# High weight tiles before low ones in each quadrant product, and query pieces cut early and used

## The chip, the cores and the metric

The kernel runs on one core of one Trainium2 chip. The metric is the device time of one execution in microseconds, as the median of several runs. TensorE (PE) multiplies matrices, and each matmul has a load of its own for its stationary operand (PEld in the profile). VectorE (DVE) and ScalarE (ACT) do element-wise work, GpSimd (POOL) a little, and SyncE (SP) issues the DMA transfers.

## The reference

A decoder trunk of two layers on 512 tokens with 1024 channels, batch 1, all in float32. Layer 0 mixes with multi-head latent attention (MLA), layer 1 with gated linear attention (GLA). Each mixer is followed by an MLP with a squared ReLU, and a last RMS norm ends the trunk:

```python
def sq_relu_mlp(xn, w_up, w_down):
    hid = jnp.square(jax.nn.relu(xn @ w_up))
    return hid @ w_down

# layer i:  x += Mixer_i(rms_norm(x));  x += sq_relu_mlp(rms_norm(x), w_up, w_down)
# w_up is 1024 x 4096, w_down 4096 x 1024
```

The GLA mixer begins with `h = rms_norm(x) @ w_in`, and the first 512 columns of `h` are its queries.

## The kernel before, in words

**Layout.** The residual stream lies transposed in SBUF: `xT[j]` holds channels 128j to 128j+127 on the partitions and the 512 tokens along the row. `first` and `second` are the token halves of 256.

**Split precision.** A float32 product is made of three matmuls in a reduced format. An operand is split into a high and a low part: `split` (L108) writes the high part as a rounded copy on ACT (L110) and the low part as source minus high part on DVE (L113). `mm3` (L115) issues high weight x high input (L118), high weight x low input (L119) and low weight x high input (L120), one after the other. `piece` (L143) makes such a pair of weight tiles, `wh` and `wl`, of 1024 columns; there are three buffers of each.

**The MLP.** Its products are made by a scheme in the manner of Strassen. The input is cut into quadrants, by channel half and token half, and each 2 x 2 block product takes seven quadrant products instead of eight. The sums and differences of quadrants that this needs are made by `QuadNorm.pair` (L281) for the normed input (its four results T1 to T4 for one pair of channel tiles), by DVE subtractions and additions on the weights, and by additions on the results. The weights go up in 8 blocks of 512 columns. `up_block` (L811) returns its steps: `s1` is the product named 11, `s2` is 21 on top of it, `s5` is T1, `s6` T2, `s3` 22, `s7` T3 and `s4` T4. Block 0 has a step `s0` that loads and cuts its first weights before the MLP begins. An up product is 4 k tiles x 2 output tiles x 3 = 24 matmuls of 256 columns into the two halves of one PSUM bank. Its loop has the output tile outside and k inside. `down_block` (L928) does the same for the way down, for the first 6 blocks: a down product is 4 k tiles x 4 output tiles x 3 = 48 matmuls, fed by two weight pieces; its input is split on the spot (`operand`, L937). `matmuls` (L797) is the loop of both. The last two blocks go down by plain products of 512 columns (`down`, L1024, or `down_final`, L1039).

**The order around the MLP.** `out_proj` (L769) closes the mixer: four steps, each with two output tiles, whose results are added to the residual (L783), scaled, split, squared and paired for the MLP. In its last step it lets the MLP run its first step `s0`. Then the MLP itself starts: two matmuls that only warm up, then the lead, which is the steps `s1`, `s2` of block 0 and `s1`, `s2` of block 1. Behind the first of them `begin` (L1077) puts the norm (`finish`, L251: one product with `acc`, the sum of squares, in float32, L253, then a reciprocal root on ACT and DVE) and four subtractions on `xT` (L1080). Behind the lead come the other steps, with down products put between them. Block 1 reads its first weights by one DMA of 1 MB into the pool `down_w` (L824), the others by DMAs of 512 KB (L829), all issued by SP.

**The GLA's start.** While the last piece of the MLP's last block is being used, `prefetch` (L1547) loads the weights of the GLA's first 256 query columns and cuts two pieces into `self.qk`. Nothing reads them. `gla` then calls `proj_qk(0)` (L1189), which loads the same columns again (L1190) and cuts them (L1191). `a_pair` (L389) multiplies: 8 k steps of 6 matmuls, with the norm issued before the sixth step. After it come the second projection, the scales per token (eight tiny matmuls, L1216) and the gates.

**What sets the order.** The program is traced in the order of the code; a scheduler then orders the instructions of each engine by priority and by what it reckons to be ready, so the matmuls of two products may be mixed. `tc.keep_in_program_order(i)` ties an instruction to the program's order on its engine, and `with tc.issue_after(i)` puts what the block traces behind `i` on `i`'s engine. Waits on data and on free buffers are added by the framework. `PADS` are unused bytes at the start of a pool, which shift the addresses behind them. Down in memory, pools that are opened after others are closed take over their space, and a tile waits for those whose bytes it takes.

## Time and profile before

| What | Value |
|---|---|
| Median of 3 runs | 1106.01 us (1104.63 to 1106.75) |
| Profiled execution | 1105.17 us, its span 1103.5 us |
| TensorE busy | 1071.4 us, 97% of the span, 7322 matmuls |
| VectorE busy | 895.1 us, 81% |
| ScalarE busy | 643.1 us, 58% |
| Mean granted TensorE clock | 0.988 |
| HBM read and written | 106.74 MB, 2.10 MB |

In a row of groups stand the line, the engine, the operation, what it writes and reads, shapes and count, then busy time and the mean of one in ns, then the idle time of the engine just before them with what ended it. A row of waits has the engine and line that waited, what it waited for, the total, the number of times and the longest. A row of the timeline has start, duration, engine, line, operation and operands, and in brackets the idle time before it with what ended it. A matmul's duration is longer than its distance to the next, as matmuls overlap; the pace is read from the starts. The 512-column matmuls of the mixers and the 256-column ones of the MLPs lie in different stretches: the MLPs run from about 190 to 475 us and from 762 to 1049 us, the GLA from about 519 us.

### The profile page before, as it was taken

How to read it: one execution, taken by the hardware profiler on the slowest of the kernel's cores; microseconds unless marked ns; L12 is line 12 of the kernel's file. 1: busy time of each engine (PE TensorE's matmuls, PEld its weight loads, DVE VectorE, ACT ScalarE, POOL GpSimd, SP SyncE). 2: the span in 40 equal slices, each digit the busy share in tenths (PEclk: the TensorE clock that was granted, in tenths of full speed). 3: DMA queues.
4: the chain of work that ended last, by engine and by line, in shares of the span. 5: the costliest groups of instructions: out<-in, count | busy, mean ns of one | idle time of the engine just before them, and what ended most of it. 6: DMA issues, size and time to landing. Idle time of an engine off the chain costs nothing.

```text
span 1103.5 us, 17836 instructions
## 1 busy us (share of the span) xinstructions
PE 1071.4 (97%) x7322; PEld 985.7 (89%) x7322; DVE 895.1 (81%) x1212; ACT 643.1 (58%) x936; POOL 44.5 (4%) x78
## 2 busy tenths in 40 slices
PE   8999999899999999998899999999999999999997
PEld 7788988899999999986688888887999999999986
DVE  6789878999899899867365654678899899799865
ACT  6576654566567676645234744655556566766734
POOL 6410000000000000030000000000000000000000
PEclk9999999999999999999799999999999999999999
DMA  7312113523432523250222212223423523422312
GB/s 215 83 48 77 39 46 99 181 78 115 154 103 90 184 85 100 92 192 0 86 77 77 77 40 76 77 77 124 145 96 99 170 77 126 154 86 95 128 45 77
DMA packets 100098, 109.98 MB, mean 100 GB/s; under 512 B 8129, under 2 KB 74961, under 8 KB 100017
## 3 DMA queue, kind: packets, MB, share of 16 engines
q1 hardware_dynamic: 98000, 107.62, 30.8%
q10 hardware_dynamic: 1952, 1.21, 0.4%
q8 instruction: 57, 0.93, 0.4%
q0 software_dynamic: 64, 0.02, 0.1%
q14 instruction: 25, 0.20, 0.1%
HBM read 106.74 MB, written 2.10 MB: 99 GB/s over the span
## 4 chain that ended last, share of the span: by engine, by line
PE 85%; DVE 10%; ACT 2%; issue 1%; DMA 0%; ACTq 0%; DVEq 0%
PE ps L118 26%; PE ps L120 26%; PE ps L119 26%; DVE wl L113 3%; PE ps L135 2%; PE ps L1342 2%; ACT wh L110 1%; DVE raw L1000 1%; DVE h L113 1%; DVE raw L884 1%; DVE set L244 1%; DVE acc L236 1%; PE ps L1379 0%; DVE raw L899 0%; PE ps L666 0%
## 5 line engine op out<-in xcount | busy, mean ns | idle before, releaser
L110 ACT ACTIVATE wh<-raw 128x1024 fp32r<-128x1024 f32 x210 | 221.4, 1058 | 180.5 <-PE ps L119 141.5
L113 DVE TENSOR_TENSOR wl<-raw,wh 128x1024 fp32r<-128x1024 f32 x210 | 255.5, 1224 | 25.4 <-ACT wh L110 24.9
L120 PE MATMUL ps<-h,wl 128*128 128x256 f32 x672 | 188.5, 281 | 2.2 <-DVE wl L113 2.2
L118 PE MATMUL ps<-h,wh 128*128 128x256 f32 x672 | 188.1, 280 | 0.0
L119 PE MATMUL ps<-h,wh 128*128 128x256 f32 x672 | 188.0, 280 | 0.0
L120 PEld LDWEIGHTS ps<-h,wl 128*128 128x128 f32 x672 | 126.5, 188 | 3.1 <-DVE wl L113 3.0
L118 PEld LDWEIGHTS ps<-h,wh 128*128 128x128 f32 x672 | 126.4, 188 | 0.0
L119 PEld LDWEIGHTS ps<-h,wh 128*128 128x128 f32 x672 | 126.4, 188 | 0.0
L110 ACT ACTIVATE wh<-wraw 128x1024 fp32r<-128x1024 f32 x43 | 44.8, 1055 | 85.2 <-PE ps L120 41.5
L118 PE MATMUL ps<-set,wh 128*128 128x512 f32 x232 | 92.7, 400 | 1.6 <-ACT set L243 1.6
L119 PE MATMUL ps<-set,wh 128*128 128x512 f32 x232 | 92.5, 399 | 0.1
L120 PE MATMUL ps<-set,wl 128*128 128x512 f32 x232 | 92.3, 398 | 0.0
L113 DVE TENSOR_TENSOR wl<-wraw,wh 128x1024 fp32r<-128x1024 f32 x43 | 52.6, 1229 | 10.8 <-ACT wh L110 10.6
L118 PE MATMUL ps<-wh,set 128*128 128x512 f32 x144 | 59.7, 414 | 0.0
L841 ACT ACTIVATE q<-q 128x512 f32<-128x512 f32 x64 | 40.1, 626 | 30.7 <-DVE q L840 30.7
L113 DVE TENSOR_TENSOR h<-q,h 128x1024 fp32r<-128x1024 f32 x42 | 51.4, 1224 | 7.9 <-ACT h L110 7.9
L120 PE MATMUL ps<-wh,set 128*128 128x512 f32 x144 | 56.3, 391 | 0.0
L119 PE MATMUL ps<-wl,set 128*128 128x512 f32 x144 | 56.2, 391 | 0.0
L118 PEld LDWEIGHTS ps<-set,wh 128*128 128x128 f32 x232 | 44.5, 192 | 10.7 <-ACT set L243 1.8
L119 PEld LDWEIGHTS ps<-set,wh 128*128 128x128 f32 x232 | 44.8, 193 | 9.9 <-DVE set L244 0.8
L120 PEld LDWEIGHTS ps<-set,wl 128*128 128x128 f32 x232 | 44.7, 193 | 9.3
L110 ACT ACTIVATE h<-q 128x1024 fp32r<-128x1024 f32 x42 | 44.1, 1049 | 0.8 <-DVE q L986 0.8
(490 smaller groups left out, 3005.8 us busy)
## 6 DMA issues: line engine op xcount, KB each, us to landing
raw<-in_mlp_w_down_dram SPq DMA_DIRECT2D x38, 1024.0 KB, 5.1
raw<-in_mlp_w_up_dram SPq DMA_DIRECT2D x62, 512.0 KB, 3.9
wraw<-in_gla_w_in_dram SPq DMA_DIRECT2D x12, 1024.0 KB, 5.1
wraw<-in_mla_w_o_dram SPq DMA_DIRECT2D x8, 512.0 KB, 4.8
wraw<-in_gla_w_o_dram SPq DMA_DIRECT2D x8, 512.0 KB, 4.8
raw<-in_mlp_w_up_dram SPq DMA_DIRECT2D x2, 1024.0 KB, 7.6
xT<-in_x_dram SPq DMA_DIRECT2D x6, 256.0 KB, 7.4
wraw_qn<-in_mla_w_uq_dram SPq DMA_DIRECT2D x6, 256.0 KB, 3.4
```

Source lines behind the costliest of these rows:

```text
L110: order(ACT.activation(hi, src, AF.Copy))
L113: lo_eng.tensor_tensor(lo, src, f(hi), ALU.subtract)
L118: PE.matmul(psum, wh, xh, start=start, stop=False, **kw)
L119: PE.matmul(psum, wh, xl, start=False, stop=False, **kw)
L120: PE.matmul(psum, wl, xh, start=False, stop=stop, **kw)
L135: PE.transpose(psum, src, ident[: src.shape[0], : src.shape[0]])
L236: DVE.tensor_tensor(self.acc, self.acc, s, ALU.add)
L244: DVE.scalar_tensor_tensor(lo, src, g, f(hi), ALU.mult, ALU.subtract)
L841: ACT.activation(qs, qs, AF.Square)
L884: DVE.tensor_tensor(s, v["a21"], v["a22"], ALU.add)
L1000: DVE.tensor_tensor(v["S"], v["12"], v["S"], ALU.subtract)
L1342: PE.matmul(p[:, t * 64 : (t + 1) * 64].rearrange("p (n c) -> p n c", c=m), k[:, sl], later, start=True, stop=True)
```

## The change

It has these parts, all around the two MLPs and the start of the GLA:

- **Order in a quadrant product.** `matmuls` issues all matmuls with the high weight tile first, for each k and output tile the high and the low input, and then all with the low weight tile. An up product goes through both output tiles inside k, where it finished one output tile first. A down product does so for each of its two pieces.
- **Products in program order.** The first matmul of each such group is kept in program order.
- **The lead.** The last pair of channel tiles is combined (`pair(3)`) not at the end of `out_proj` but in block 1's first step, behind the cut of that step's weights. The norm goes from behind block 0's `s1` into its `s2`, before that result is finished, with its matmul kept in order. The four subtractions go behind the lead. Block 1's first weights are loaded before the lead, by two DMAs of 512 KB instead of one of 1 MB.
- **Helpers.** `split` returns its DVE instruction, and `piece` keeps it in the list `cut_at`.
- **The GLA.** `proj_qk(0)` uses the two pieces that `prefetch` cut; the second load and cut are gone.
- **A pad** of 224 bytes in front of the pool `down_w`.

```diff
-    PADS = dict(stage=224, right=64, up=448, masks=256, keep=128)
+    PADS = dict(stage=224, right=64, up=448, masks=256, keep=128, down_w=224)
...
+    cut_at = []
...
-        split(raw, hi, lo, order=order)
+        cut_at.append(split(raw, hi, lo, order=order))
...
-            nxt.pair(c)
+            if c < 3:
+                nxt.pair(c)
...
-            for k in ks:
-                for m in ms:
-                    mm3(
...
+            def one(i, j, k, m, start, stop):
+                return PE.matmul(
+                    p[:, m * TH : (m + 1) * TH],
+                    w[i][:, k - k0, m * P : (m + 1) * P],
+                    x[k][j],
...
+            steps = [(k, m) for k in ks for m in ms]
+            for k, m in steps:
+                i = one(0, 0, k, m, begin and k == 0 and m % 2 == 0, False)
+                if (k, m) == steps[0]:
+                    tc.keep_in_program_order(i)
+                one(0, 1, k, m, False, False)
+            for k, m in steps:
+                one(1, 0, k, m, False, end and k == 3)
...
                 if b == 1 and half == 0:
...
+                    return ahead[trail]
...
-                for j in range(2):
-                    matmuls(p, w, 0, range(KH), [j], quad[name], begin, True)
+                matmuls(p, w, 0, range(KH), range(2), quad[name], begin, True)
...
+                if b == 1:
+                    v["11"] = piece(a, KH, 256)
+                    with tc.issue_after(cut_at[-1].ins):
+                        nrm.pair(KH - 1)
                 product(v["x1"], a, "11", True)
...
                 product(v["x1"], v["a12"], "21", False)
+                if b == 0:
+                    nrm.finish(tc.keep_in_program_order)
                 finish(pairs(v["x1"]), 0, first)
...
-        opened("down_w")
+        pad(opened("down_w"), PADS["down_w"])
...
+        t = wide_raw().rearrange("p a (b n) -> p (a b) n", b=2)
+        ahead = t[:, :KH], t[:, KH:]
+        for i, a in enumerate(ahead):
+            SP.dma_start(a, w_up[i * 512 : i * 512 + 512, FB : FB + 256].rearrange("(k p) n -> p k n", p=P))
         lead = [blocks[b].pop(0) for b in (0, 0, 1, 1)]
-        for i, step in enumerate(lead):
+        for step in lead:
             step()
-            if i == 0:
-                begin()
+        with tc.issue_after(cut_at[-1].ins):
+            for k in range(KH):
+                DVE.tensor_tensor(xT[k][:, second], xT[k][:, second], xT[k + KH][:, second], ALU.subtract)
...
-            raw = col_chunk(w_in, c * 256, 256)
-            w = [piece(raw[:, :, j * P : (j + 1) * P], ND, P) for j in range(2)]
+            if c == 0:
+                w = nrm.qk
+            else:
+                raw = col_chunk(w_in, c * 256, 256)
+                w = [piece(raw[:, :, j * P : (j + 1) * P], ND, P) for j in range(2)]
```

More of the change, by code (lines that the diff above doesn't have):

```diff
@@ L249, in add, with finish @@
             self.square(src)
-        def finish(self):
+        def finish(self, order=lambda i: i):
             m = bank("c")
-            PE.matmul(m, self.inv, self.acc, start=True, stop=True)
+            order(PE.matmul(m, self.inv, self.acc, start=True, stop=True))
             r = sb.tile([P, S], F32, tag="rstd", bufs=1, name=uname("rstd"))
@@ L1075, in down_final @@
                         nxt.row(t, c, ps_[c])
-        def begin():
-            nrm.finish()
-            for k in range(KH):
-                DVE.tensor_tensor(xT[k][:, second], xT[k][:, second], xT[k + KH][:, second], ALU.subtract)
         blocks = [up_block(b) for b in range(NB)]
```

19 lines of the change are left out of this document (5 added, 14 removed).

## The prediction, on record before the changed kernel was run

> **What bounds the kernel now.** I read the page first, then TensorE's waits, then the stretches round each place that the change touches.
>
> ```profile
> PE 1071.4 (97%) x7322; PEld 985.7 (89%) x7322; DVE 895.1 (81%) x1212; ACT 643.1 (58%) x936; POOL 44.5 (4%) x78
> ...
> PE 85%; DVE 10%; ACT 2%; issue 1%; DMA 0%; ACTq 0%; DVEq 0%
> ...
> L113 DVE TENSOR_TENSOR wl<-raw,wh 128x1024 fp32r<-128x1024 f32 x210 | 255.5, 1224 | 25.4 <-ACT wh L110 24.9
> ```
>
> TensorE (PE) is the bound, and where the chain of work that ended last leaves it, it goes through VectorE (DVE, 10%), mostly to make the low weight tile `wl`, 1.22 us each. The matmuls' waits, in total us, times, longest:
>
> ```profile
> PE ps L120 <- DVE wl L113: 7.4, 7, 1.8
> PE ps L253 <- DVE acc L236: 4.3, 1, 4.3
> PE ps L118 <- ACT wh L110: 3.6, 4, 1.0
> PE ps L1216 <- DVE rstd L219: 3.6, 1, 3.6
> ```
>
> L120 is the low-tile matmul: it waits for the very thing that the new order asks for later. L253 and L1216 are the norm and the token scales at the start of the GLA. The stretches, in order the length, busy time (and instructions) of PE, its weight loads, DVE, ACT, POOL, then the granted clock:
>
> ```profile
> 190.40:244.30 53.90, 48.97 (x390) 47.04 (x389) 49.00 (x53) 30.60 (x39) 0.00 (x0) 0.97 0.46 149
> 762.20:816.50 54.30, 49.06 (x389) 47.04 (x389) 49.32 (x54) 30.48 (x39) 0.00 (x0) 0.97 0.45 146
> 244.30:475.10 230.80, 228.52 (x1971) 227.91 (x1970) 216.79 (x197) 154.01 (x174) 5.37 (x10) 1.00 0.36 115
> 816.50:1048.90 232.40, 230.73 (x1970) 230.00 (x1970) 216.32 (x196) 154.81 (x175) 0.00 (x0) 1.00 0.36 116
> 275.00:300.00 25.00, 25.00 (x220) 25.00 (x220) 22.20 (x20) 15.28 (x19) 0.00 (x0) 1.00 0.52 169
> 975.00:1000.00 25.00, 24.95 (x213) 24.75 (x212) 24.25 (x22) 16.59 (x19) 0.00 (x0) 1.00 0.39 125
> 518.70:543.90 25.20, 17.33 (x57) 13.11 (x57) 9.54 (x13) 6.91 (x11) 0.00 (x0) 0.73 0.20 53
> ```
>
> The first two rows are the leads of the two MLPs (from the first up product to the first down product), the next two the rest of them. An undisturbed stretch does 220 matmuls of 256 columns in 25 us, 113.6 ns each; another only 213, 117.4 ns. A lead holds 16 products of 24 such matmuls: 16 x 24 x 113.6 ns = 43.6 us, with the norm and two warming matmuls some 44.6. The leads are 9.3 and 9.7 us longer than that. The rest has 42 up and down products per MLP, 1968 matmuls, 223.6 us at that pace: 7.2 and 8.8 us over. The last row is the GLA's start: 25 us at 17.3 busy and a mean clock of 0.73. These are the places where anything can be won. DVE is busy 94% of the third row, so it is nearly a second bound.
>
> **The change part by part. GLA start.** Today the query pieces are cut during the last down product and thrown away; the projection loads and cuts them again.
>
> ```profile
> 507.87 1.06 ACT L110 ACTIVATE wh<-raw 128x1024 fp32r<-128x1024 f32 x1
> ...
> 510.56 1.05 ACT L110 ACTIVATE wh<-raw 128x1024 fp32r<-128x1024 f32 x1
> ...
> 526.49 1.04 ACT L110 ACTIVATE wh<-wraw 128x1024 fp32r<-128x1024 f32 x1
> ...
> 521.65 0.75 DVE L244 SCALAR_TENSOR_TENSOR set<-xT,gains,set 128x512 fp32r<-128x512 f32 x1 [0.79 <-ACT set L243]
> ...
> 496.06 0.39 PE L120 MATMUL ps<-hh,wl 128*128 128x512 f32 x1
> ...
> 518.50 0.39 PE L120 MATMUL ps<-hh,wl 128*128 128x512 f32 x1
> 523.15 2.05 PE L253 MATMUL ps<-acc,inv 128*128 128x512 f32 x2 [4.25 <-DVE acc L236]
> 528.81 1.86 PE L1216 MATMUL ps<-one_t,rstd 1*128 1x1 f32 x8 [3.62 <-DVE rstd L219]
> ...
> 531.19 0.63 PE L119 MATMUL ps<-set,wh 128*128 128x512 f32 x1
> 531.62 0.63 PE L118 MATMUL ps<-set,wh 128*128 128x512 f32 x1
> ...
> 543.73 0.39 PE L118 MATMUL ps<-set,wh 128*128 128x512 f32 x1
> ```
>
> The pieces at 507.87 and 510.56 are the unused ones; the used ones are cut at 526.49, behind the norm, and PE, with the projection ordered behind norm and scales, stands still after 518.7 and then runs at 430 ns a matmul. Full pace is (518.50 - 496.06) / 99 intervals = 227 ns. With the early pieces the 48 query matmuls can start at 518.7: the sixth of eight k steps comes 6.8 us later with the norm before it, and the last token tile (521.65 + 0.75 = 522.4) is there. 518.7 + 48 x 0.227 + 0.75 for the norm (193.61 to 194.36 in the lead) = 530.4, against 543.73: 13.3 us. The scales (1.86) come later instead: 11.5 sure, 13.3 at best. **I take 12.** The pieces now hold two of three `wh` buffers till 530.4; the second must wait until the last but one down piece frees its own, about 513. The next projection's first piece finds the buffer freed at 518.7 and its second is cut while 24 matmuls (5.4 us) run: nothing added. The dropped 1 MB load and two cuts were hidden and free 2.4 us of DVE.
>
> **The leads.** Here are moved: the cut of block 1's first piece ahead of the last T tile (`pair(3)`: two ACT, five DVE instructions), the norm behind block 0's second product, four subtractions behind the lead, and block 1's load (now two DMAs) ahead of block 0's second pair.
>
> ```profile
> 187.91 0.39 SPq L824 DMA_DIRECT2D raw<-in_mlp_w_up_dram  x1
> ...
> 190.67 0.69 DVE L783 TENSOR_TENSOR xT<-ps,xT 128x512 f32<-128x512 f32 x1 [1.19 <-PE ps L120]
> ...
> 195.00 0.48 DVE L290 SCALAR_TENSOR_TENSOR raw<-xT,gains,raw 128x256 f32<-128x256 f32 x1
> ...
> 197.00 1.23 DVE L113 TENSOR_TENSOR T3l<-raw,T3h 128x1024 fp32r<-128x1024 f32 x1
> ...
> 199.47 1.22 DVE L113 TENSOR_TENSOR wl<-raw,wh 128x1024 fp32r<-128x1024 f32 x1
> ...
> 193.61 1.12 PE L253 MATMUL ps<-acc,inv 128*128 128x512 f32 x2
> 194.36 0.49 PE L118 MATMUL ps<-x4h,wh 128*128 128x256 f32 x1
> ...
> 198.49 0.39 PE L118 MATMUL ps<-x0h,wh 128*128 128x256 f32 x1 [0.93 <-ACT wh L110]
> ...
> 200.75 0.39 PE L120 MATMUL ps<-x0h,wl 128*128 128x256 f32 x1 [1.75 <-DVE wl L113]
> ```
>
> The piece waited for at 198.49 and 200.75 stands behind `T3l` at 199.47 on DVE. Its DMA is out at 187.91 and SP holds nothing in front of it that it must pass but the second pair's load; both land before PE asks (two first products, 190.7 + 5.7 + 0.75 = 197). Cut first, its low tile can be ready near 194.5, and both waits go. Late next is `T3l`: four short DVE instructions like the one at 195.00 and its own 1.23, some 3 us, due in the last k quarter of T1's high half, which begins after four products: 190.5 + 4 x 2.8 + 0.75 = 202.5, so near 204. If that cover failed, T1 would wait for it, at most 2 us. The bounds: nothing, or PE's 9.3. But DVE works 49.0 of 53.9 us there, so the lead shortens by its idle 4.9, by the 1.1 of a cut put into the idle 1.19 before 190.67, and by what the low tiles are asked for later (after 16 matmuls instead of 2, 14 x 0.1136 = 1.6): 7.6 at most. Part of that idle is DVE waiting for ACT. **I take 6 each, 12 in all.**
>
> **The order inside a product.** A product keeps its 24 or 48 matmuls and weight loads. In the rest of the MLPs the waits are like this one:
>
> ```profile
> 355.02 0.28 PE L119 MATMUL ps<-T0l,wh 128*128 128x256 f32 x1
> 356.04 0.39 PE L120 MATMUL ps<-T0h,wl 128*128 128x256 f32 x1 [0.75 <-DVE wl L113]
> ```
>
> The start is 1.02 us late where 0.11 is due, after a wait of 0.75: some 0.27 for the restart. Of the seven L120 waits two of up to 1.75 are in the leads; five remain with 7.4 - 3.5 = 3.9 us, with restarts 5.3. The 1.6 us of slack covers each alone; as DVE is 94% busy some come back. From 0 to 5.3, **I take 4.4.** `wh` is also let go after two thirds of a product, so ACT's copies, which are no bound (58%), start earlier.
>
> Against it stands the pace. Up products run all of one output half and then the other; after the change they alternate halves, as down products do after every three matmuls. A down and an up product side by side, in undisturbed time (48 and 24 matmuls; the counts hold some that overlap the edges):
>
> ```profile
> 291.31:296.92 5.61, 5.61 (x51) 5.61 (x50) 3.00 (x3) 2.69 (x4) 0.00 (x0) 1.00 0.67 233
> 296.92:299.64 2.72, 2.72 (x27) 2.72 (x25) 2.52 (x3) 2.01 (x2) 0.00 (x0) 1.00 0.85 265
> ```
>
> 116.9 ns and 113.3 ns. Over both MLPs, 4704 matmuls outside and inside the leads, all at 113.6 instead of the present 116 or so (230.80 less 3 of stalls over 1968) would win 10; all at 117.4 would lose 6. **I take a loss of 2.5**, near the down row. The `down_w` padding moves addresses only; the matmul kept in order per product issues nothing.
>
> **Sum.** The profiled execution took 1105.17 us for a span of 1103.5; the median is 1106.01, 0.8 above it. 1105.2 - 12 - 12 - 4.4 + 2.5 = 1079.3; on the median 1080.1, so **1080**.
>
> **The rivals.** *DVE is the bound.* The leads and later waits come back as DVE waits elsewhere, and only the GLA start stays: 1106 - 12 + 0 to 2 = 1095. For: 49.0 of 53.9 and 216.79 of 230.80 us busy. Against: 14 us idle in that long stretch, so work can be caught up.
>
> *The early pieces don't free PE.* The norm and scales are still put ahead of the queries, PE waits till 530.6 and only the cut is gone; then about 1.5 of the 12 stays: 1090. For: today's order. Against: that order has the pieces cut late, and these are cut by 514.
>
> *The pace falls with the order.* With a new weight address and another half at each low matmul the stream slows; this is the case that ends slower. The gains are 28.4, so over 4704 matmuls it decides from 6 ns more, 122 ns or 205 in 25 us; at 200 in 25 us, 125 ns, the time is 1106 - 28.4 + 4704 x 9 ns = 1120. For: 213 against 220 shows that the pace isn't fixed. Against: loads are one for each matmul already (7322 of both), and switching halves costs at most 3.6 ns in the down row.
>
> *The pace rises* to 113.6 throughout, with fewer disturbances: 1106 - 28.4 - 10 = 1068. The Trainium skill (TensorE: Matmul & The Clock Gate, Back-to-back issue gap) gives 262 cycles of 2.4 GHz for 256 columns, 109 ns: by that the same case would end about 1047. No row here is under 113.
>
> **How the numbers follow.** Forecast 0.62, DVE-bound 0.15, pieces late 0.09, pace up 0.08, pace down 0.04, and 0.02 for a mix of the bad ones near no change. The forecast's own terms (GLA 11.5 to 13.3, leads 4 to 15, waits 0 to 5.3, pace -10 to +6) make 1068 to 1092 likely; with the DVE case inside, **1066 to 1095** leaves some 2 in 10 out. Faster, by over 0.2% (2.2 us, about what a measurement tells from no change), in all but the last two: 0.94; same 0.01; slower 0.05.
>
> **What would show it.** The query matmuls begin by 519 without a wait, at 227 ns, and the norm stands between them. PE has no wait for `wl` over 0.3 us in block 1's first product, and a lead shrinks to 46 to 50 us. The total of L120's waits falls under 3 us. In a stretch after the lead 25 us hold 213 to 217 matmuls. Wrong are the steps if the leads stay near 54 us with DVE full, if the norm still precedes the queries, or if quiet stretches hold under 210.

## The result

The changed kernel takes **1095.91 us** (median of 4 runs, 1095.63 to 1096.2) against 1105.6 for the kernel before on the same chip: ratio 0.9916, 95% interval 0.99 to 0.9932. That is 9.7 us faster; 26 were forecast. The profiled execution took 1096.2 us, with a span of 1094.5.

The page of the changed kernel, its line of engines, its chain and the group of the low weight tiles:

```profile
PE 1070.8 (98%) x7322; PEld 988.7 (90%) x7322; DVE 891.5 (81%) x1210; ACT 641.7 (59%) x934; POOL 44.1 (4%) x78
...
PE 90%; DVE 5%; ACT 2%; DMA 2%; issue 1%; SPq 0%; DVEq 0%; ACTq 0%
...
L113 DVE TENSOR_TENSOR wl<-raw,wh 128x1024 fp32r<-128x1024 f32 x210 | 253.9, 1218 | 25.5 <-ACT wh L110 24.5
```

The same view of TensorE's waits (total us, times, longest):

```profile
PE ps L802 <- DVE q L926: 6.0, 4, 1.9
PE ps L802 <- ACT wh L110: 3.3, 2, 1.6
PE ps L802 <- ACT mt L876: 1.5, 2, 0.7
PE ps L802 <- ACT ps L882: 1.3, 2, 0.7
...
PE ps L802 <- DVE wl L113: 0.9, 2, 0.5
```

The waits for `wl` fell from 7.4 to 0.9 us, and those of the norm and the scales (4.3 and 3.6) are gone. But there are new ones: the T4 products, which follow T3 in the program's order and go into the same bank, wait for the sum `q` that still reads it (L926), and others wait for evacuations and high tiles on ACT. L802 is every matmul of the MLP products now.

The same stretches as before: both leads, both rests, the first 25 us of the queries, two quiet stretches (length; busy time and instructions of PE, weight loads, DVE, ACT, POOL; granted clock):

```profile
191.56:247.46 55.90, 49.43 (x389) 47.72 (x388) 48.92 (x56) 31.25 (x40) 0.00 (x0) 0.97 0.28 86
753.53:808.10 54.57, 48.00 (x390) 46.21 (x389) 48.75 (x56) 31.02 (x40) 0.00 (x0) 1.00 0.29 88
247.46:479.24 231.78, 231.78 (x1971) 231.78 (x1970) 216.33 (x197) 154.53 (x175) 5.43 (x8) 1.00 0.36 114
808.10:1039.87 231.77, 231.77 (x1971) 231.77 (x1969) 216.33 (x196) 155.38 (x176) 0.00 (x0) 1.00 0.36 117
522.79:547.79 25.00, 25.00 (x112) 19.58 (x111) 14.49 (x20) 8.93 (x13) 0.00 (x0) 1.00 0.19 53
300.00:325.00 25.00, 25.00 (x215) 25.00 (x214) 23.63 (x23) 15.83 (x17) 0.00 (x0) 1.00 0.38 119
900.00:925.00 25.00, 25.00 (x215) 25.00 (x214) 24.90 (x23) 17.49 (x20) 0.00 (x0) 1.00 0.30 86
```

Set against the stretches that the prediction shows:

| stretch | before | after | difference |
|---|---|---|---|
| up to the first MLP | 190.47 | 191.56 | +1.1 |
| first lead | 53.90 | 55.90 | +2.0 |
| rest of the first MLP | 230.8 | 231.8 | +1.0 |
| plain down part, GLA, to the second MLP | 287.0 | 274.3 | -12.8 |
| second lead | 54.3 | 54.6 | +0.2 |
| rest of the second MLP | 232.4 | 231.8 | -0.6 |
| what is left | | | +0.1 |
| span | 1103.5 | 1094.5 | -9.0 |

The GLA's start gave all that was forecast, and the granted clock there is 1.00 where it was 0.73. The 1.1 us ahead of the first MLP arise near 15 us of the span, in a wait of 0.9 us behind the first loads, which the change does not touch; over all traces of this study that part takes 190.5 to 193.2 us. The leads did not shrink at all. In the rests PE is busy without a gap (231.78 of 231.78), so every wait is gone, and yet they take as long as before. These two are the questions for the experiments.

The granted clock bears on the leads. In the changed kernel's first lead (0.97) one wait is followed by a stretch at half the clock, in which matmuls start some 213 ns apart where 118 ns is usual:

```profile
221.94 0.39 PE L802 MATMUL ps<-T0h,wh 128*128 128x256 f32 x1 [1.89 <-DVE q L926]
...
222.70 0.42 PE L802 MATMUL ps<-T1h,wh 128*128 128x256 f32 x1
222.92 0.41 PE L802 MATMUL ps<-T1l,wh 128*128 128x256 f32 x1
223.13 0.41 PE L802 MATMUL ps<-T1h,wh 128*128 128x256 f32 x1
```

The stretch is 3.41 us long, so it costs some 1.7 us, and the second lead has none (1.00). Before, each lead had one (0.97 in both rows of the prediction), at the wait of 1.75 us for `wl`. In the leads of all the traces such a stretch begins within 1.5 us of the end of a PE wait of 1.6 to 2.9 us, but waits of up to 2.5 us bring none in other leads; what decides it, no run here shows. So the length of a lead has to be read together with its clock.

The query matmuls stand directly behind the last down matmul, and the norm (L255) stands between them:

```profile
522.56 0.39 PE L120 MATMUL ps<-hh,wl 128*128 128x512 f32 x1
522.79 0.39 PE L118 MATMUL ps<-set,wh 128*128 128x512 f32 x1
...
529.36 0.39 PE L120 MATMUL ps<-set,wl 128*128 128x512 f32 x1
529.59 1.02 PE L255 MATMUL ps<-acc,inv 128*128 128x512 f32 x2
530.05 0.80 PE L118 MATMUL ps<-set,wh 128*128 128x512 f32 x1
```

### The profile page after: what moved, and what is told of

It reads as the page before. It is cut to its first block, busy times and chain, and to the rows that moved or that the text cites. A ratio compares the mean times of both kernels' runs of the same rounds, so it can differ in the third digit from the quotient of the medians.

```text
span 1094.5 us, 17834 instructions
## 1 busy us (share of the span) xinstructions
PE 1070.8 (98%) x7322; PEld 988.7 (90%) x7322; DVE 891.5 (81%) x1210; ACT 641.7 (59%) x934; POOL 44.1 (4%) x78
## 4 chain that ended last, share of the span: by engine, by line
PE 90%; DVE 5%; ACT 2%; DMA 2%; issue 1%; SPq 0%; DVEq 0%; ACTq 0%
PE ps L802 47%; PE ps L118 12%; PE ps L119 12%; PE ps L120 12%; PE ps L1356 2%; PE ps L135 1%; DVE wl L113 1%; DMA wraw_ckv<-in_mla_w_in_dram 1%; ACT wh L110 1%; DMA raw<-in_mlp_w_up_dram 1%; PE ps L1393 0%; DVE q L845 0%; PE ps L1362 0%; PE ps L1342 0%; PE ps L668 0%
## 5 line engine op out<-in xcount | busy, mean ns | idle before, releaser
L802 PE MATMUL ps<-h,wh 128*128 128x256 f32 x1344 | 172.2, 280 | 0.0
L802 PEld LDWEIGHTS ps<-h,wh 128*128 128x128 f32 x1344 | 164.5, 188 | 0.0
L802 PE MATMUL ps<-h,wl 128*128 128x256 f32 x672 | 92.7, 280 | 0.0
L802 PEld LDWEIGHTS ps<-h,wl 128*128 128x128 f32 x672 | 85.1, 188 | 0.0
L113 DVE TENSOR_TENSOR wl<-wraw,wh 128x1024 fp32r<-128x1024 f32 x41 | 50.3, 1229 | 10.7 <-ACT wh L110 10.5
L119 PEld LDWEIGHTS ps<-set,wh 128*128 128x128 f32 x232 | 44.0, 190 | 10.7 <-DVE set L246 1.6
L802 PE MATMUL ps<-T0h,wh 128*128 128x256 f32 x128 | 33.8, 287 | 9.3 <-DVE q L926 6.0
L118 PE MATMUL ps<-hh,wh 128*128 128x512 f32 x96 | 37.4, 389 | 0.0
```

The costliest lines, as they stand in the source:

```text
L113: return lo_eng.tensor_tensor(lo, src, f(hi), ALU.subtract)
L118: PE.matmul(psum, wh, xh, start=start, stop=False, **kw)
L119: PE.matmul(psum, wh, xl, start=False, stop=False, **kw)
L802: return PE.matmul(p[:, m * TH : (m + 1) * TH], w[i][:, k - k0, m * P : (m + 1) * P], x[k][j], start=start, stop=stop, skip_group_check=True,)
```

## The experiments

Three theories were put against each other. *Order*: the new order inside the products, or the rule that products keep the program's order, costs PE time in the leads and slows its pace. *DVE*: DVE bounds the leads, as a rival in the prediction has it. *Arrangement*: the moved pair, norm and transfers make the leads longer. A ratio is always to the kernel before, with its 95% interval. The spacing of quiet matmuls is worked out from their start times, all intervals under 135 ns from the first down product on. The runs lie on several chips and at several times, where the kernel before took 1103.8 to 1106.5 us; two times of different runs are therefore compared by their ratios too.

### The parts, one by one

**The early pieces alone**, on the kernel before:

```diff
+            if c == 0:
+                w = nrm.qk
```

> The kernel before with one edit alone: the first query projection uses the pieces that the prefetch cut. Theory: this is the whole of the gain; TensorE goes from the last down product straight to the query matmuls, 12 to 13 us less, so 1093, which would be faster than the changed kernel by 2 to 3 us, and the rest of the change costs that. Rival: the GLA's start wins only in company with the new order; 1100 or more.

1092.18 us, ratio 0.9883 (0.9866 to 0.99). In its trace the way from the last down matmul to the second MLP takes 230.8 us (519.55 to 750.31) against 243.5 (518.73 to 762.24) before. The pieces alone are worth as much as forecast, and alone they are faster than the whole change, by 3.7 us, though the two intervals touch. So the rest of the change costs time.

**The changed kernel without the pieces:**

```diff
-            if c == 0:
-                w = nrm.qk
```

> The changed kernel without the early query pieces: the first projection loads and cuts its own weights again behind the norm. With the pieces alone the kernel before gained 14 us (12 were forecast). If that holds in company of the rest too, 1106 to 1112, above the kernel before; if the new order makes the GLA's start shorter by itself, 1098 to 1104.

1109.38 us, ratio 1.0028 (1.0015 to 1.0041): 13.5 us above the changed kernel (12.4 by the ratios), and slower than before. The waits of the kernel before are back:

```profile
PE ps L255 <- DVE acc L238: 4.3, 1, 4.3
PE ps L1227 <- DVE rstd L221: 3.6, 1, 3.6
```

The GLA term stands, with or without the other parts.

**The changed kernel without the program order of products:**

```diff
-                if (k, m) == steps[0]:
-                    tc.keep_in_program_order(i)
```

> The changed kernel without keeping each product's first matmul in program order; all else stays. Theory 'order': in the lead of the changed kernel T4 stands right behind T3 and waits for the sum at L926 that reads T3's bank (1.89 and 1.06 us in the first MLP, 6.0 us in all four); set free, other products' matmuls fill these waits, the two leads shrink from 55.9 and 54.6 us to 52 or less, and the time falls by 4 to 6 us. Rival 'DVE': the lead ends when VectorE's 49 us of work and its own waits are through; the leads stay within 1 us, and so does the time.

1095.77 us, ratio 0.9913 (0.9895 to 0.9931); leads 55.65 and 54.30, spacing 117.64 and 117.90 ns. Nothing changes: the kept program order is not the cause.

**The changed kernel with the old order inside the products** (high, high, low of each k step), the rest kept:

```diff
-            steps = [(k, m) for k in ks for m in ms]
+            up = len(ms) == 2
+            steps = [(k, m) for m in ms for k in ks] if up else [(k, m) for k in ks for m in ms]
...
-            for k, m in steps:
                 one(1, 0, k, m, False, end and k == 3)
```

> The changed kernel with the old order inside a product (high-high, high-low, low-high for each tile, up products one half after the other), first matmul still in program order. Theory 'order sets the pace': undisturbed up products go back from 2.82 to 2.72 us and down products from 5.66 to 5.61, and the waits for the low tile come back with some 6 us; the time stays within 3 us of the changed kernel's. Rival 'state': the pace is a state that the stream falls into at its start and keeps when nothing disturbs it; products stay at 2.83 until a wait comes, and the time rises by 4 us or more.

1104.08 us, ratio 0.9978 (0.9966 to 0.999): the high-first order is worth some 8 us in company of the rest. The leads grow by 3 and 3.6 us (58.83 and 58.21, the granted clock 0.94 in both, so some 1.7 and 3.4 us of it are the clock) and waits return to the rest. The spacing is 116.5 and 116.6 ns in up products and 116.8 and 117.0 in down products, so the pace depends on the order too, by about 1 ns. The order theory has lost half of its ground: the new order helps.

**The same with the products free to move:**

```diff
-                if (k, m) == steps[0]:
-                    tc.keep_in_program_order(i)
```

> The changed kernel with the old order inside the products and without the wait for the program's order: the new lead and the pieces alone. If the new lead costs by itself, leads of 56 us or more and 1094 to 1100 us, above the 1092.2 of the pieces alone. If it was the program order that made the three-by-three run dear (1104.1, leads near 58.5), the leads come back to 54 and the time to about 1092.

1100.88 us, ratio 0.9948 (0.9932 to 0.9965): 8.7 us above the pieces alone (7.2 by the ratios). New lead and old order together cost.

**High first, but one output half after the other:**

```diff
+            steps = [(k, m) for m in ms for k in ks] if up else [(k, m) for k in ks for m in ms]
```

> The changed kernel, high tiles still first, but in up products one output half after the other within the high and within the low part; down products unchanged. Theory 'halves': alternating the output half is what slows the stream, so up products go from 2.82 to 2.72 us while down products stay at 5.66, and the time falls by 8 to 10 us. Rival 'low tiles in a row' or 'state': up products stay at 2.82, and the time stays within 1 us.

1095.21 us, ratio 0.991 (0.9891 to 0.9928). The spacing is 117.3 in up and 116.7 in down products: the change of halves is not what makes the up products slow.

**The kernel before with pieces and high-first order, old lead** (this loop without the program order):

```diff
+            for k, m in steps:
+                one(0, 0, k, m, begin and k == 0 and m % 2 == 0, False)
+                one(0, 1, k, m, False, False)
+            for k, m in steps:
+                one(1, 0, k, m, False, end and k == 3)
```

> The kernel before, with the early query pieces and the high-first order inside the products; the lead, the transfers and the free order stay those of before. If the new lead arrangement is what costs (the sum, the late pair and the program order on DVE and PE), this run keeps the 14 us of the pieces, loses the waits for wl (some 4 us) and shows leads near 51 us: 1082 to 1088 us. If the high-first order itself slows the quiet matmuls (117.6 ns against 113.6 in the up products), it gains the waits and gives them back: 1091 to 1095 us with up spacing near 117.6.

1084.5 us, ratio 0.9796 (0.9771 to 0.9822): 11 us faster than the whole change. The leads are 51.54 and 54.19 (clock 1.00 and 0.97); the up products run at 117.8 ns in the first MLP and at 114.1 in the second. So high-first does not need the new lead, and it does not force the slow pace throughout.

**The changed kernel with all three parts of the lead undone** (pair, norm with its subtractions, transfers; program order kept), the edits of the next three runs together:

```diff
-            if c < 3:
-                nxt.pair(c)
+            nxt.pair(c)
...
+                nrm.finish()
...
-                    return ahead[trail]
```

> The changed kernel with all three parts of the lead undone (pair, norm and subtractions, transfers), so only the pieces, the high-first order and the program order of the products are left. Against the 1084.5 of the same without the program order: if the program order costs, 1089 to 1096; if it costs nothing, 1082 to 1088.

1085.2 us, ratio 0.9831 (0.9813 to 0.985). Not to be told from the run without the program order, as the intervals overlap; leads 52.13 and 52.13, the clock 1.00 in both. **The arrangement of the lead costs 10.7 us** (9.4 by the ratios).

### Which part of the arrangement

**The pair back at its old place:**

```diff
-            if c < 3:
-                nxt.pair(c)
+            nxt.pair(c)
...
-                    with tc.issue_after(cut_at[-1].ins):
-                        nrm.pair(KH - 1)
```

> The changed kernel with the fourth pair of the norm where it stood before (ahead of the lead, not behind block 1's first pieces). The kernel with the old lead and the high-first order took 1084.5, the changed one 1095.9: 11 us that the lead's new arrangement must have cost, in the lead (4.4 us in the first MLP) and in the quiet pace (117.6 against 113.6 in the up products). If the late pair is what does it, 1086 to 1090 and a lead under 53 us in the first MLP; if it is not, 1094 to 1098.

1089.44 us, ratio 0.9869 (0.9843 to 0.9895). More than half of it, but not all. Leads 53.34 and 54.90 (clock 1.00 and 0.97), and the pace is no longer fixed: 117.8 ns in the up products of the first MLP, 114.3 in those of the second.

**Norm and subtractions back:**

```diff
-                if b == 0:
-                    nrm.finish(tc.keep_in_program_order)
...
-        for step in lead:
+        for i, step in enumerate(lead):
             step()
-        with tc.issue_after(cut_at[-1].ins):
-            for k in range(KH):
+            if i == 0:
+                nrm.finish()
+                for k in range(KH):
```

> The changed kernel with the norm's scale and the four subtractions of the second half of xT straight behind the lead's first step, as before. If moving these is the cause, 1086 to 1090; if it is not, 1094 to 1099 (the subtractions then stand ahead of the lead's sums on DVE, as in the kernel before).

In this kernel the late fourth pair reads its second half after the subtractions, so the numbers in its tiles differ; the instructions are the same. 1093.08 us, ratio 0.9895 (0.9874 to 0.9915), leads 53.11 and 54.55 (clock 1.00 and 0.97), spacing 117.64 and 117.90 as in the changed kernel. A small part, between the two expectations.

**The transfers back:**

```diff
-                    return ahead[trail]
+                    if not trail:
+                        t = wide_raw().rearrange("p a (b n) -> p (a b) n", b=2)
+                        SP.dma_start(t, w_up[:, c0 : c0 + 256].rearrange("(k p) n -> p k n", p=P))
+                        v["a12"] = t[:, KH:]
+                    return t[:, :KH]
```

> The changed kernel with block 1's first tile loaded in one transfer from within the block, as before, in place of two transfers ahead of the lead. If the place of these transfers matters, 1086 to 1092; if not, 1095 to 1097.

1101.01 us, ratio 0.9968 (0.9955 to 0.9982): slower by 5.1 us, which neither expectation has. With the late pair, the early transfers are needed.

**Pair and norm back, transfers kept early:**

```diff
-            if c < 3:
-                nxt.pair(c)
+            nxt.pair(c)
...
+                nrm.finish()
```

> The changed kernel with pair and norm (with its subtractions) where they were, but block 1's transfers still ahead of the lead. Undoing only the transfers made it slower by 5.1 us; undoing all three parts made it 10.7 us faster. If the early transfers are good in themselves, this is faster than the 1085.2 with all three undone: 1078 to 1084. If their worth came from the late pair and norm alone, 1084 to 1088.

1084.45 us, ratio 0.9806 (0.9783 to 0.9829). The transfers by themselves bring nothing that can be told from the 1085.2 without them. This is, with the old lead above, the fastest kernel of the study: 11 us below the changed one, 21 below the one before.

The leads of these kernels in the same view. The first lead with the pieces alone, and with all three parts undone:

```profile
191.39:245.58 54.19, 48.95 (x390) 46.97 (x388) 49.12 (x53) 30.50 (x39) 0.00 (x0) 0.97 0.45 147
...
190.67:242.80 52.13, 47.94 (x389) 46.27 (x388) 49.49 (x54) 31.14 (x40) 0.00 (x0) 1.00 0.48 153
```

With pair and norm back, transfers early:

```profile
190.89:242.58 51.69, 47.14 (x389) 45.69 (x388) 49.49 (x54) 31.15 (x40) 0.00 (x0) 1.00 0.48 155
747.40:799.06 51.66, 47.14 (x389) 45.68 (x388) 49.48 (x54) 31.13 (x40) 0.00 (x0) 1.00 0.48 155
```

The changed kernel with the transfers back:

```profile
193.12:251.15 58.03, 50.87 (x390) 48.90 (x389) 48.78 (x56) 31.03 (x40) 0.00 (x0) 0.94 0.27 83
757.24:815.15 57.91, 50.55 (x390) 48.52 (x389) 48.78 (x56) 31.03 (x40) 0.00 (x0) 0.94 0.26 82
```

DVE works 48.8 to 49.5 us in every one of them. What differs is how long it idles: 2.2 us with pair and norm back, 7.0 and 5.8 in the changed kernel, 9.2 with the transfers back. With pair and norm early, the lead is as long as DVE's work and little more. PE's idle time is 4.5 us with pair and norm back, 6.5 and 6.6 in the changed kernel, 7.2 and 7.4 with the transfers back. The rest of the difference is mostly the clock: with the transfers back it is 0.94 in both leads, which costs some 3.4 us each. The changed kernel has 0.97 and 1.00, so the clock is most of what the one with the transfers back loses against it in the leads. Where DVE idles in the changed kernel stands in its timeline (start, length, instruction, in brackets the idle time before it and what ended it):

```profile
193.49 0.75 DVE L276 SCALAR_TENSOR_TENSOR x7l<-xT,gains,x7h 128x512 fp32r<-128x512 f32 x1 [0.79 <-ACT x7h L275]
194.16 0.69 DVE L238 TENSOR_TENSOR acc<-acc,tmp 128x512 f32<-128x512 f32 x1
196.40 1.23 DVE L113 TENSOR_TENSOR wl<-raw,wh 128x1024 fp32r<-128x1024 f32 x1 [1.55 <-ACT wh L110]
...
199.80 0.48 DVE L292 SCALAR_TENSOR_TENSOR raw<-xT,gains,raw 128x256 f32<-128x256 f32 x1
201.63 0.69 DVE L218 SCALAR_TENSOR_TENSOR mt<-ps,mt 128x512 f32<-128x512 f32 x1 [1.35 <-ACT mt L129]
...
205.11 1.22 DVE L113 TENSOR_TENSOR T3l<-raw,T3h 128x1024 fp32r<-128x1024 f32 x1
```

And ACT, which ended these three idle times and twice stood behind PE itself:

```profile
194.82 0.58 ACT L882 ACTIVATE ps<-ps 128x512 f32<-128x512 f32 x1 [0.84 <-PE ps L802]
195.31 2.00 ACT L110 ACTIVATE wh<-raw 128x1024 fp32r<-128x1024 f32 x2
199.44 0.69 ACT L129 ACTIVATE mt<-ps,eps_t 128x512 f32<-128x512 f32 x1 [2.13 <-PE ps L255]
```

With the pair early, DVE has its work there (`raw`, the sums, `T3l` at 197.42) and no idle time from 191.8 to 204:

```profile
193.89 0.48 DVE L291 SCALAR_TENSOR_TENSOR raw<-xT,gains,raw 128x256 f32<-128x256 f32 x1
194.28 1.22 DVE L890 TENSOR_TENSOR raw<-raw,raw 128x1024 f32<-128x1024 f32 x1
195.42 0.48 DVE L292 SCALAR_TENSOR_TENSOR raw<-xT,gains,raw 128x256 f32<-128x256 f32 x1
195.82 0.48 DVE L293 SCALAR_TENSOR_TENSOR raw<-xT,gains,raw 128x256 f32<-128x256 f32 x1
196.21 1.22 DVE L918 TENSOR_TENSOR raw<-raw,raw 128x1024 f32<-128x1024 f32 x1
197.42 1.22 DVE L113 TENSOR_TENSOR T3l<-raw,T3h 128x1024 fp32r<-128x1024 f32 x1
```

So the piece that is "cut first" is not cut sooner: ACT makes its high tile only behind the evacuation of the first product (L882, 194.82), and DVE, whose filler was moved away, stands idle for 3.7 us. That work then comes on top, later. DVE's subtraction for T2 (L910) begins at 208.42, 16.9 us into the lead; in the kernel before it began at 204.20, 13.7 us into it. ACT can cut T2's high tile only behind that and behind the evacuation of T1, at 210.19. So PE waits inside T1 and ahead of T2, where neither the kernel before nor the one with pair and norm back has a wait:

```profile
208.44 0.50 PE L802 MATMUL ps<-T0h,wl 128*128 128x256 f32 x2 [0.47 <-DVE wl L113]
...
211.29 0.39 PE L802 MATMUL ps<-T0h,wh 128*128 128x256 f32 x1 [1.63 <-ACT wh L110]
```

The waits for `q` (2.9 us in this lead) are no part of the difference: they are 2.9 us with pair and norm back as well.

**Does DVE bound the changed lead?** Its eight sums in each lead are left out (the products then run on tiles as loaded):

```diff
-                DVE.tensor_tensor(s, v["a21"], v["a22"], ALU.add)
+                if b > 1:
+                    DVE.tensor_tensor(s, v["a21"], v["a22"], ALU.add)
```

(likewise the three subtractions in `s6`, `s3` and `s7`)

> The changed kernel without the eight sums of weight tiles on DVE in each lead (of blocks 0 and 1, some 1.22 us each, 9.8 us of DVE): this leaves out part of the computation, the products of the lead run on tiles as loaded. If DVE, 88% busy there, is what keeps the changed lead at 55.9 and 54.6 us, the leads come down to 48 to 50 us and the time to 1082 to 1087. If it is the places of the pieces and evacuations in the order, PE waits as long without the sums: leads of 53 us or more and 1091 to 1096.

1089.83 us, ratio 0.9852 (0.983 to 0.9874); leads 51.72 and 51.69, between the two expectations. The lead gets 4.2 and 2.9 us back, 1.7 of the first by the clock (1.00 in both). DVE's work inside it falls by 6.5 and 6.4 us of the 9.8, to 42.4. DVE is thus part of the bound and not all of it: PE, busy 47.6 us of the 51.7, then still waits, most of all for the sums of results and for evacuations.

### The pace

**A short matmul ahead of each T1 product:**

```diff
+                n = 64 + 32 * (b % 5)
+                PE.matmul(v["x5"][:, :n], x[:, :P], x[:, :n], start=True, stop=True, skip_group_check=True)
```

> The changed kernel with one more matmul of 64 to 192 columns ahead of each T1 product, into a bank that the product then starts afresh: 32 short matmuls more, some 2 us of work, and nothing else changed. If the quiet spacing of 117.6 and 117.9 ns is a state that an undisturbed stream keeps, and a break can leave, the spacing of some products moves to 113 to 115 (or to 120) after a kick and the mean changes by 1 ns or more: 1085 to 1100. If the spacing comes from the order and the tiles, it stays at 117.6 and 117.9 and the time is 1097 to 1099.

1101.37 us, ratio 0.9955 (0.9937 to 0.9974). Spacing 117.4 and 117.7 in up, 117.9 in down products: no kick shifts it. The time is more than expected, as the leads grew to 57.08 and 56.95.

**A wait in each MLP:**

```diff
+                if b == 4:
+                    d = sb.tile([P, 64], F32R, tag="late", bufs=1, name=uname("late"))
+                    ACT.activation(d, v["b2"][:, :64], AF.Copy)
+                    tc.keep_in_program_order(PE.matmul(v["x5"][:, :64], quad["T1"][0][0][:, :P], d, start=True, stop=True, skip_group_check=True))
```

> The changed kernel with one wait put into each MLP some 30 to 40 us behind the lead: a matmul of 64 columns ahead of block 4's T1 product that must wait for ACT to copy 64 columns of a sum written just before. It costs 1 to 2 us per MLP. If the quiet pace is a state that a wait of PE can change and that then stays, spacing after the wait is another than 117.6 and 117.9 ns in at least one MLP (113 and 117 at best, which would give some 5 us back per MLP). If the pace belongs to the changed kernel's order and tiles, it is 117.6 and 117.9 before and after the wait, and the time 1097 to 1100.

1102.94 us, ratio 0.9972 (0.9961 to 0.9984). PE waits 1.9 us ahead of 325.3 and of 889.5 us; but for the two up products at the wait, the up products before and behind it take 2.81 to 2.84 us and the down products 5.64 to 5.67. The time is more than expected; the rests are 2.3 and 2.4 us longer, and the second lead (55.77) has a half-clock stretch that it lacks in the changed kernel. A pace that a wait could switch is not what the changed kernel has.

**Without the new pad ahead of the wide raw tiles:**

```diff
-    PADS = dict(stage=224, right=64, up=448, masks=256, keep=128, down_w=224)
+    PADS = dict(stage=224, right=64, up=448, masks=256, keep=128, down_w=0)
```

> The changed kernel without the new pad of 224 bytes ahead of the ring of wide raw tiles, so that all later tiles of that stack move by 224 bytes per partition. If the spacing hangs on where the tiles lie against each other, up or down spacing moves by 1 ns or more (5 us or more of the whole time). If not, 1095 to 1097 with 117.6 and 117.9.

1095.93 us, ratio 0.9908 (0.9887 to 0.9929); 117.64 and 117.90. This pad does nothing.

After these runs one thing stood out. With the order of the change inside the products, each kernel with the late pair kept 117.64 and 117.90 (117.4 to 117.75 and 117.9 where matmuls were put in), and each with the early pair did not; yet PE's order of matmuls is the same in the changed kernel and in the one with the pair back. By the layout of the stack, the tiles of the fourth pair are made behind the pad of 448 bytes if the pair is late, ahead of it if it is early: T3h and T3l lie 448 bytes further on in the stack ("higher" from here on) in the changed kernel. By the same layout, nothing else that a matmul touches lies elsewhere. Two runs change this address alone; in each of them PE, DVE and ACT run the same instructions in the same order as in the kernel that it is set against.

**The changed kernel with the two tiles at their old address, the pair cut as late as ever:**

```diff
             if c < 3:
                 nxt.pair(c)
+            else:
+                nxt.late = nxt.room(c)
```

(`room` makes the two tiles, and `pair` then fills them)

> The late pair has a second effect that the diff does not name: the tiles of the fourth pair, T3h and T3l, are now made after the pad of 448 bytes in their stack and lie 448 bytes higher than before; nothing else that TensorE reads or writes moves, and its order of instructions is the same with the pair early or late. In all runs with the late pair (but for the two that also changed the order within a product) the quiet pace was 117.64 and 117.90 ns, kick or wait or not; in all with the early pair it changed between some 113.3 and 117.9. This is the changed kernel with room for the two tiles made ahead of the pad, so at the old addresses; the pair is cut as late as in the changed kernel. If the addresses set the pace, the spacing leaves 117.64 and 117.90 (down products at 116.6 to 117.3, up products at 113.3 to 117.9 by stretches), with the lead still near 55: 1087 to 1094. If it is the late cut itself, 117.64 and 117.90 stay and 1095 to 1097.

(There were three such runs with another order within a product, not two.)

1092.18 us (1089.99 to 1093.6), ratio 0.9882 (0.9864 to 0.99), with leads of 55.64 and 54.72: faster by 3.7 than the changed kernel, though the two intervals touch. Its spacing is 113.7 and 114.0 ns in up products, 117.1 and 117.2 in down products.

**The fast kernel with the two tiles 448 bytes higher, the pair early:**

```diff
+            if k == 3:
+                pad(pool, 448)
...
-    PADS = dict(stage=224, right=64, up=448, masks=256, keep=128, down_w=224)
+    PADS = dict(stage=224, right=64, up=0, masks=256, keep=128, down_w=224)
```

> The kernel with pair and norm where they were and the transfers ahead (1084.45) with the pad moved from behind T3h and T3l to right ahead of them, so that they lie 448 bytes higher, as in the changed kernel; the pair is cut early. If the addresses set the pace, the spacing is 117.64 and 117.90 ns throughout both MLPs, the leads stay near 51.7, and the time is 1085 to 1090 with a narrow spread; if not, up products at 113.3 to 117.9 by stretches and 1082 to 1086.5 as without the shift.

1088.57 us (1088.07 to 1090.36), ratio 0.9856 (0.9834 to 0.9878), with leads of 51.64 and 51.81: slower by 4.1 than without the shift (5.5 by the ratios). Its spacing is 117.64 and 117.90 in both MLPs.

The starts of products one behind the other, from the timelines. The changed kernel:

```profile
301.17 0.28 PE L802 MATMUL ps<-x4h,wh 128*128 128x256 f32 x1
...
304.00 0.28 PE L802 MATMUL ps<-T0h,wh 128*128 128x256 f32 x1
...
306.82 0.28 PE L802 MATMUL ps<-h,wh 128*128 128x256 f32 x1
...
312.48 0.28 PE L802 MATMUL ps<-T0h,wh 128*128 128x256 f32 x1
```

The same with the old address:

```profile
301.14 0.28 PE L807 MATMUL ps<-x4h,wh 128*128 128x256 f32 x1
...
303.87 0.28 PE L807 MATMUL ps<-T0h,wh 128*128 128x256 f32 x1
...
306.59 0.28 PE L807 MATMUL ps<-h,wh 128*128 128x256 f32 x1
...
312.20 0.28 PE L807 MATMUL ps<-T0h,wh 128*128 128x256 f32 x1
```

The fast kernel with the new address, the rests of its MLPs:

```profile
242.22:474.00 231.78, 231.78 (x1971) 231.78 (x1970) 216.34 (x197) 154.44 (x175) 5.44 (x8) 1.00 0.36 114
800.11:1031.88 231.77, 231.77 (x1970) 231.77 (x1969) 216.33 (x196) 155.43 (x176) 0.00 (x0) 1.00 0.36 117
```

In the changed kernel an up product takes 2.83 and 2.82 us (24 matmuls), a down product 5.66 (48). At the old address it is 2.73, 2.72 and 5.61, most of the time. With the new address the fast kernel gets the rests of the changed one, 231.78 and 231.77, to a hundredth of a us. That the address bears on the pace is shown in either direction: at the new one, with the high-first order, only 2.82 and 5.66 occur. Why 448 bytes in two tiles that only a part of the products reads slow all products, down products too, no run here shows.

At the old address the pace takes one of two values. After some waits it goes to 2.83 for an up product, with 5.60 for a down product, and may come back; the first MLP of the kernel with old lead and high-first order stayed at 2.83 for 230 us. The fast kernel without the shift also ran at 2.83 in nearly the whole of its first MLP, whose rest is 1.3 us shorter than with the shift, and at 2.72 in about half of its second, whose rest is 1.9 us shorter. With it the runs of these kernels scatter (1081.98 to 1086.45, against 1095.63 to 1096.2 of the changed kernel). What chooses between the two values there stays open.

## Why the prediction was right and where it was wrong

**GLA start: right.** Forecast -12 (11.5 to 13.3); measured -12.8 in the trace, 14 us for the pieces alone, 13.5 in company of the rest. The norm stands between the query matmuls and all start without a wait. They start at 522.8 and not by 519, as all that goes before is 4.1 us later.

**The leads: this step failed.** Forecast 6 us less each, measured 2.0 and 0.2 more. The two waits at which the step aimed, 0.93 and 1.75 us at block 1's first product, did go. What failed is the step from there to the length, "so the lead shortens by its idle 4.9": DVE's idle time was taken as a store to be used up, and the move enlarged it to 7.0 us. "Cut first, its low tile can be ready near 194.5" was wrong as well: DVE began that tile at 196.40, because its high tile stood on ACT behind the evacuation of the first product. The step named what is late next (`T3l`, near 204, at a cost of 2 us at most); it was there at 206.3, and T1 did not wait for it. What the step did not ask is what DVE would do in the place that the pair had filled: nothing, for 3.7 us, and the delay came out as the waits of 0.47 and 1.63 us at T1 and T2.

Two things are in the measured number. The high-first order shortens the leads from 54.2 and 54.3 with the pieces alone to 52.13 each, 2.1 us; some 1.7 us of this are the clock, 0.97 with the wait of 1.75 us and 1.00 without it. The moved pair and norm then add 4.2 and 2.9 (51.69 and 51.66 against 55.90 and 54.56), of which PE's waits are 1.9 and 2.0 and, in the first, a new half-clock stretch 1.7. The clock had no term in the prediction, though its rows show 0.97 in both leads.

**The waits in the rest: right.** All are gone, 0 of 231.78 us idle, where PE's idle time had been 2.3 and 1.7 us.

**The pace: right in its sign, short in its size.** "25 us hold 213 to 217 matmuls" is what came (215 and 215). The term was +2.5; the waits forecast at -4.4 and the pace made together -1.9, and measured is +0.3 (463.2 to 463.5). So the pace took back all of what the waits had given, some 4.3 us. Its cause was not the order alone, as the rival "pace falls with the order" has it, but the address of two tiles, which moved with the pair and which no step of the prediction looked at. With the old address and the same order the rests are 3.2 and 2.1 us shorter than in the changed kernel; at the new address the old order within a product runs about 1 ns faster than the new one.

**The sum.** 1079.3 by steps, 1096.2 in the profiled execution. The difference of 16.9 is 14.2 from the leads, 2.2 from the rests, 1.1 from the first loads, less 0.8 from the GLA's start, within 0.2. Two of the prediction's readings were wrong with little weight: the rest of an MLP holds 61 products (40 up, 21 down), not 42, for the same 1968 matmuls; and a start 1.02 us behind the one before, where 0.11 is due, is 0.91 late, so the restart behind a wait of 0.75 is 0.16 us and not 0.27, and the upper bound of the waits 4.7 and not 5.3.

**The rivals.** The rival "DVE is the bound" gave 1095, and the time is that, but partly by luck: the leads that grew by 2.2 us and the 1.1 us of the first loads are not in it. It is half right: its waits did not come back "elsewhere" in the rests, which have none. In the leads DVE's work of some 49 us looks like a floor, and the kernels with pair and norm at their old places, transfers early or not, come within 2.7 us of it; but without the sums the lead is still 51.7 with DVE at 42.4, so PE and its waits are a second floor close behind. "Early pieces do not free PE" is excluded: 12 to 14 us. "Pace falls with the order" is excluded as the whole cause: the high-first order with the early pair and low address runs at 113.3 to 114.3 ns for long stretches, and at 117.8 in others.

The forecast of "faster" was right; its range ended at 1095, below the time, since it gave the leads no room to grow.

## What to carry to other kernels

When work is moved off the front of a stretch whose busiest engine is nearly full, ask what that engine will do in the gap: here the moved pair had been the filler, and its idle time rose from 2.2 to 7 us. Try the parts of a change one by one when they touch the same stretch: pieces and high-first order alone take 1084.5, and the arrangement that was added to them takes 11 us back. A wait of PE can cost more than its length: here 1.75 and 1.89 us were each followed by a stretch at half the clock, some 1.7 us more. And when a tile is made at another place in the program, look at where it now lies: an address may cost as much as a wait.

## What the runs showed of the hardware

The spacing of 256-column matmuls, each with a weight load of its own, is 113.3 to 120 ns as the mean of a product, in stretches without any wait and at a granted clock of 1.00. With the high-first order it comes in a few steady values: 2.72 us for an up product with 5.61 for a down product, 2.83 with 5.60, 2.82 with 5.66. Moving two operand tiles by 448 bytes chose the last of them throughout, and neither short matmuls nor a wait of 1.9 us brought another of them from there. The Trainium skill (TensorE: Matmul & The Clock Gate, section Back-to-back issue gap) gives 262 cycles of 2.4 GHz, 109 ns, for 256 columns, as the gap of an isolated matmul; no stretch here reached it. That an address changes the spacing was not expected; what in it counts stays open.

In the leads the granted clock fell to a half for 3.41 us, or twice that, at PE waits of 1.6 to 2.9 us, with matmuls some 213 ns apart, and not at every wait of that length. The two leads of one kernel, which do the same work, differ by this: by 1.3 us in the changed kernel (55.90 and 54.57), which has one such stretch in the first.
